# Two softmax mixers of a fused two-stack block: weight low parts from GpSimd to VectorE, the row division from VectorE to ScalarE

## The chip, the cores and the metric

One Trainium2 chip, one core of it. The metric is the device time of one execution of the whole program in microseconds (us). TensorE (PE) does the matmuls, VectorE (DVE), ScalarE (ACT) and GpSimd (POOL) the element-wise work, and SyncE's queue (SP) starts the transfers of the weights.

## The reference

Two stacks of residual blocks run one after the other on a sequence of 256 tokens with 1024 features, batch 1, in float32. The second stack, where the change sits, has four layers. Each layer is a half-weighted gated feed-forward block, an attention mixer, and a second feed-forward block. The mixers of the four layers are, in order, stick-breaking ("sb"), "moba", "mla" and stick-breaking again. With 256 tokens there is one block only, so moba is causal softmax attention with partly rotated queries and keys; mla builds queries and keys through low-rank matrices. Of both mixers what matters here is, for each of 16 heads:

```
logits = q @ k.T * scale            # masked: key position <= query position
p = softmax(logits, axis=-1)        # exp(logits - rowmax) / rowsum
o = p @ v
mix = concat(o) @ w_o
```

## The kernel before

Activations lie transposed, features on partitions. A float32 product is made of three matmuls on parts that TensorE takes at one pass each (`mm3`, lines 343 to 345): high weight part by high activation part, high by low, and low by high. So each weight tile of 128x128 needs two derived tiles. The weights come in chunks of 16 tiles (1 MB) through SP's queue into four buffers named `raw`. Units of 8 tiles are then split: ScalarE rounds `raw` to the high part `whi` (`_hi`, line 295), and a second engine makes the low part `wlo = raw - whi` (`_lo`, line 305). Five buffers each hold `whi` and `wlo`. When the matmuls start a new unit, `ahead` issues the high part of the unit three further on and the low part of the unit two further on (LA is 3). Which engine makes the low part is chosen by `lo_pool`: 0 is VectorE always, 1 is GpSimd always, 2 is every other unit on GpSimd.

A mixer handles two heads at a time, eight pairs in all. `attention` plays an order written out by hand in each slot s (`SLOT`, the entry without a name for moba and mla): `p0 n2 p1 m2 p2 s1 f3`. Here p0 and p1 are the projections of pair s (query and key), n2 is the division by the row sums for pair s-2 (`softmax2`), m2 its transposes on TensorE and the split of the result into `ph` and `pl`, p2 the evacuation of the projections (for moba with the rotation, lines 819 to 823), s1 the scores of pair s-1 and the first half of its softmax (`softmax1`: row maxima on VectorE, four exponentials with row sums on ScalarE into `p` and `sm`), and f3 the product with the values for pair s-3, whose result is split into `xs`. After the eight slots an order named `TAIL` ends the last pairs and begins the output projection. At its first "w" step lo_pool is set to 0 and LA to 1.

The program names the operations in this order; the queue of each engine holds them in nearly this order and runs strictly one after another. An operation that waits holds up all that stands behind it on its engine.

`softmax2` takes one reciprocal of the row sums (128x4) on VectorE (line 869) and then four multiplications by a column of it (line 873): per head 256 columns for the second half of the queries and 128 for the first half. The transposes (line 892) read their result.

Of the kernel before, what the change touches and what calls it, by code (L numbers as in the profile page):

```python
# [12 lines left out]
AF = mybir.ActivationFunctionType  # L13
ALU = mybir.AluOpType
# [194 lines left out]
class Net:  # L209
# [41 lines left out]
    def banks_for(self, attention):  # L251
        one, two = self.ps1, self.ps2
        lin = one[:3] if attention else one
        self.rings = {"lin": lin, "pv": one[3:], "sc": two}
# [612 lines left out]
    def softmax2(self, pool, p, sm):  # L867
        nc = self.nc
        nc.vector.reciprocal(sm, sm)
        for i, sl in enumerate((slice(0, 256), slice(256, 384))):  # L870
            n = sl.stop - sl.start
            for j in range(2):
                nc.vector.tensor_scalar(p[:, j, sl], p[:, j, sl], sm[:, i, j:j + 1], None, op0=ALU.mult)  # L873
        return p

    def softmax2_diff(self, pool, p, sm, l):
# [102 lines left out]
    def attention(self, pool, kind, np_, proj, done, l=0):  # L979

        st = {}
        oset = done
        scale = {"diff": 0.125, "moba": 0.125, "mla": 96 ** -0.5, "sb": 1.0}[kind]

        def score(i):
            qk, rope = st["qk", i]
            if kind == "sb":
                st["sc", i] = self.sb_scores(qk)
                st["sp", i] = self.sb_soft(pool, st["sc", i])
            else:  # L990
                sc = self.scores(i, qk, rope)
                st["p", i] = self.softmax1(pool, sc, scale)

        def norm(i):
            if kind == "diff":
                st["p", i] = self.softmax2_diff(pool, *st["p", i], l)
            elif kind != "sb":
                st["p", i] = self.softmax2(pool, *st["p", i])

        def mid(i):  # L1000
            if kind == "sb":
                st["P", i] = self.sb_tail(pool, st["sc", i], st["sp", i])
            else:
                st["P", i] = self.transposes(pool, i, st["p", i], 1 if kind == "diff" else 2)

        def fin(i):
            if kind == "diff":
                st["o", i] = self.pv_diff(pool, st["P", i], i)
            else:
                oset[i] = self.pv(st["P", i], i)  # L1010

        def sub(i):
            oset[4 + i] = self.subln(*st["o", i], l)

        part = {}

        def w_o(m, upto, tag=None):
            if m not in part:
                b = self.bank(tag) if tag != "sc" else None
                if tag == "sc":  # L1020
                    b = self.bank("sc", 2)[:, 0]
                w, u = [], []
                for _ in range(8):
                    w.append(self.wtile())
                    u.append(self.cur)
                part[m] = [b[:, :S], 0, w, u]
            b, k, w, _ = part[m]
            while k < upto:
                self.mm3(b, w[k], *oset[k], k == 0, k == 7)
                k += 1  # L1030
            part[m][1] = k

        steps = {"n": norm, "f": fin, "m": mid, "s": score, "u": sub}

        def play(order, s):

            for o in order.split():
                if o[0] == "p":
                    proj(s, int(o[1]), st)
                elif o[0] == "v":  # L1040
                    self.vsteps[int(o[1])]()
                elif o[0] == "w":
                    if self.LA > 1:
                        self.lo_pool, self.LA = 0, 1
                    w_o(int(o[1]), int(o[2]), {"": "lin", "s": "sc"}[o[3:]])
                elif s >= int(o[1]):
                    steps[o[0]](s - int(o[1]))

        self.lo_pool = 2 if kind == "diff" else 1
        for s in range(np_):  # L1050
            play(SLOT.get(kind, SLOT[""]), s)
        la = self.LA
        play(TAIL.get(kind, TAIL[""]), np_)
        self.LA = la
        for m in range(8):
            w_o(m, 8, "lin")
            if m < 4:

                first = part[m + 1][3][part[m + 1][1]] if m < 3 else self.cur
                self.ahead(first + 4, first + 3)  # L1060
            self.add_x(m, part[m][0], 1.0)
# [288 lines left out]
```

## Time and profile before

| what | value |
|---|---|
| median of three runs | 2715.5 us (2712.95 to 2717.55) |
| profiled execution | 2710.43 us, its span on the core 2708.7 us |
| busy in the span: PE, DVE, ACT, POOL | 96%, 70%, 51%, 21% |
| mean granted TensorE clock | 0.985 of full speed |
| read from memory | 449.83 MB, 166 GB/s over the span |

The profile takes one execution. Its span is the time from the first to the last instruction on the core. The busy shares are averages over stages that have different limits, so the stages of the two mixers have to be read by themselves. The moba mixer lies at about 1380 to 1495 us of the span, the mla mixer at about 1890 to 1996 us.

### The profile page before, as it was taken

What the parts mean: (1) busy time and instruction counts of PE and PEld (TensorE: products, weight loads), DVE (VectorE), ACT (ScalarE), POOL (GpSimd) and SP (SyncE); (2) the same over time, 40 slices, a digit from 0 to 9 for tenths busy, and PEclk for the clock granted to TensorE, in tenths of its full rate; (3) what the DMA queues carried; (4) which work ended last, traced back from release to release, by engine and by line L of the source; (5) the groups of instructions that cost most, each with busy time, mean ns of one, the idle gap of its engine ahead of it and who ended that gap; (6) DMA issues with size and microseconds to landing.
All of it is one profiled execution on the core that took longest, in us unless ns stands there. A gap on an engine that the chain in (4) does not pass through costs nothing. (4 is left out here: it accounts for less than half of the span.)

```text
span 2708.7 us, 50918 instructions
## 1 busy us (share of the span) xinstructions
PE 2606.3 (96%) x21376; PEld 2547.6 (94%) x21376; DVE 1886.2 (70%) x2615; ACT 1392.5 (51%) x2094; POOL 573.4 (21%) x526
## 2 busy tenths in 40 slices
PE   7899998999999999999998999999899999999998
PEld 6799998999999999999987999999689999989998
DVE  8986599766766576666668765666886666656764
ACT  6544475544544764444445544554554444458553
POOL 6241253313102520010142201002320010143000
PEclk9999999999999999999998999999899999999999
DMA  5255543555555435555542555555235555542552
GB/s 206 98 198 187 172 163 121 191 188 178 173 187 199 141 129 185 187 185 187 192 171 79 176 186 187 185 191 183 71 139 187 186 183 186 188 164 98 196 187 94
DMA packets 64357, 454.15 MB, mean 168 GB/s; under 512 B 7168, under 2 KB 7680, under 8 KB 9984
## 3 DMA queue, kind: packets, MB, share of 16 engines
q1 hardware_dynamic: 63072, 448.16, 47.8%
q8 instruction: 167, 2.74, 0.4%
q0 software_dynamic: 480, 1.57, 0.2%
q10 hardware_dynamic: 576, 1.17, 0.1%
q14 instruction: 62, 0.51, 0.1%
HBM read 449.83 MB, written 1.05 MB: 166 GB/s over the span
## 5 line engine op out<-in xcount | busy, mean ns | idle before, releaser
L295 ACT ACTIVATE whi<-raw 128x1024 fp32r<-128x1024 f32 (+1 forms) x854 | 896.9, 1053 | 765.2 <-PE bank L344 381.0
L305 DVE TENSOR_TENSOR wlo<-raw,whi 128x1024 fp32r<-128x1024 f32 (+1 forms) x787 | 984.3, 1252 | 435.4 <-ACT whi L295 434.5
L343 PE MATMUL bank<-xs,whi 128*128 128x256 f32 x4480 | 1261.7, 282 | 17.8 <-ACT xs L436 16.2
L344 PE MATMUL bank<-xs,whi 128*128 128x256 f32 x4480 | 1261.8, 282 | 13.3 <-DVE xs L437 13.3
L345 PE MATMUL bank<-xs,wlo 128*128 128x256 f32 x4480 | 1260.4, 282 | 3.6 <-DVE wlo L305 3.6
L343 PEld LDWEIGHTS bank<-xs,whi 128*128 128x128 f32 x4480 | 846.5, 189 | 23.1 <-ACT xs L436 18.1
L344 PEld LDWEIGHTS bank<-xs,whi 128*128 128x128 f32 x4480 | 849.4, 190 | 19.0 <-DVE xs L437 17.4
L345 PEld LDWEIGHTS bank<-xs,wlo 128*128 128x128 f32 x4480 | 848.4, 189 | 4.4 <-DVE wlo L305 4.1
L345 PE MATMUL bank<-fh,wlo 128*128 128x256 f32 x1408 | 394.8, 280 | 0.0
L344 PE MATMUL bank<-fl,whi 128*128 128x256 f32 x1408 | 394.8, 280 | 0.0
L343 PE MATMUL bank<-fh,whi 128*128 128x256 f32 x1408 | 394.8, 280 | 0.0
L345 PEld LDWEIGHTS bank<-fh,wlo 128*128 128x128 f32 x1408 | 269.6, 191 | 0.0
L344 PEld LDWEIGHTS bank<-fl,whi 128*128 128x128 f32 x1408 | 264.3, 188 | 0.0
L343 PEld LDWEIGHTS bank<-fh,whi 128*128 128x128 f32 x1408 | 264.3, 188 | 0.0
L445 POOL TENSOR_TENSOR sqt<-x 128x256 f32<-128x256 f32 x124 | 120.4, 971 | 430.0 <-DVE x L668 281.0
L305 POOL TENSOR_TENSOR wlo<-raw,whi 128x1024 fp32r<-128x1024 f32 x67 | 167.5, 2507 | 149.6 <-ACT whi L295 148.2
L442 POOL TENSOR_TENSOR sqacc<-x 128x256 f32<-128x256 f32 x18 | 12.7, 708 | 875.7 <-DVE x L668 663.7
L369 ACT ACTIVATE fh<-act_t 128x256 fp32r<-128x256 f32 x176 | 73.5, 418 | 200.2 <-DVE act_t L727 199.3
L721 DVE TENSOR_TENSOR ffn_t<-bank,rstd 128x512 f32<-128x512 f32 x176 | 121.6, 692 | 64.3 <-PE bank L345 63.9
L344 PE MATMUL bank<-hl,whi 128*128 128x256 f32 x512 | 142.6, 279 | 0.0
L343 PE MATMUL bank<-hh,whi 128*128 128x256 f32 x512 | 142.6, 279 | 0.0
L345 PE MATMUL bank<-hh,wlo 128*128 128x256 f32 x512 | 142.6, 279 | 0.0
(285 smaller groups left out, 2852.9 us busy)
## 6 DMA issues: line engine op xcount, KB each, us to landing
raw<-in_ffn SPq DMA_DIRECT2D x264, 1024.0 KB, 4.8
raw<-in_w SPq DMA_DIRECT2D x100, 1024.0 KB, 4.9
raw<-in_mix SPq DMA_DIRECT2D x59, 1024.0 KB, 4.8
raw<-in_w SPq DMA_DIRECT2D x4, 512.0 KB, 5.6
out_dram<-x SPq DMA_DIRECT2D x4, 256.0 KB, 2.5
raw<-in_w SPq DMA_DIRECT2D x2, 256.0 KB, 4.3
x<-in_xT ACTq DMA_DIRECT2D x2, 256.0 KB, 6.3
x<-in_xT POOLq DMA_DIRECT2D x2, 256.0 KB, 6.5
```

The costliest lines, as they stand in the source:

```text
L295: self.nc.scalar.activation(hi[:, :n * 128], raw, AF.Copy)
L305: eng.tensor_tensor(lo[:, :n * 128], raw, hi[:, :n * 128].bitcast(F32), op=ALU.subtract)
L343: mm(out, lhsT=wh, rhs=xh, start=first, stop=False, **k)
L344: mm(out, lhsT=wh, rhs=xl, start=False, stop=False, **k)
L345: mm(out, lhsT=wl, rhs=xh, start=False, stop=last, **k)
L369: nc.scalar.activation(hi, src, AF.Copy)
L442: eng.tensor_tensor(sq, x, x, op=ALU.mult)
L445: eng.tensor_tensor(t, x, x, op=ALU.mult)
L721: nc.vector.tensor_tensor(t, b, self.rstd[:, None, :].to_broadcast([128, 2, S]), op=ALU.mult)
```

## The change

In `softmax2` the four multiplications by the reciprocal row sums go from VectorE to ScalarE, as a copy with a scale taken from a column (one scale for each partition); the reciprocal stays on VectorE. In `attention` the choice of `lo_pool` changes: mixers of the first stack ("diff") keep 2, stick-breaking keeps 1, and moba and mla get 0 where they had 1, so that VectorE makes every low part there. `softmax2` is called for moba and mla alone.

```
             for j in range(2):
-                nc.vector.tensor_scalar(p[:, j, sl], p[:, j, sl], sm[:, i, j:j + 1], None, op0=ALU.mult)
+                nc.scalar.activation(p[:, j, sl], p[:, j, sl], AF.Copy, scale=sm[:, i, j:j + 1])
         return p
...
-        self.lo_pool = 2 if kind == "diff" else 1
+        self.lo_pool = {"diff": 2, "sb": 1}.get(kind, 0)
         for s in range(np_):
             play(SLOT.get(kind, SLOT[""]), s)
```

## Rows read from the trace of the kernel before

**Rows 1.** Windows: length, busy us (instructions) of PE, PEld, DVE, ACT, POOL; clock, DMA, GB/s

```profile
1000.00:1380.00 380.00, 379.20 (x3179) 377.18 (x3178) 249.30 (x314) 184.21 (x251) 30.96 (x33) 1.00 0.55 189
1380.00:1495.00 115.00, 102.94 (x746) 92.44 (x745) 85.83 (x152) 56.69 (x123) 41.48 (x19) 0.94 0.30 102
1890.00:1996.00 106.00, 89.62 (x684) 79.08 (x684) 84.88 (x180) 54.28 (x132) 30.31 (x20) 0.90 0.21 73
```

**Rows 2.** Waits of PE, 1400 to 1492 us (moba): us in total, times, longest

```profile
PE pair L892 <- DVE p L873: 8.5, 7, 2.4
```

**Rows 3.** Waits of PE, 1900 to 1992 us (mla)

```profile
PE pair L892 <- DVE p L873: 7.5, 8, 1.9
PE bank L343 <- DVE qkt L1182: 4.8, 1, 4.8
```

**Rows 4.** Windows of moba's slots, cut where TensorE ends a pair's projections

```profile
1412.50:1422.90 10.40, 7.94 (x71) 7.31 (x70) 9.11 (x16) 6.13 (x14) 5.40 (x3) 1.00 0.31 102
1422.90:1463.00 40.10, 32.97 (x225) 29.37 (x225) 31.75 (x56) 19.20 (x51) 15.16 (x7) 0.83 0.23 79
1463.00:1472.70 9.70, 8.79 (x76) 8.03 (x73) 9.15 (x18) 6.03 (x14) 1.23 (x1) 1.00 0.32 110
1466.90:1475.90 9.00, 9.00 (x78) 8.32 (x77) 8.46 (x19) 6.05 (x14) 0.00 (x0) 1.00 0.27 86
```

**Rows 5.** Windows of mla: its entry, the first scores, the slots after them

```profile
1901.30:1921.30 20.00, 12.31 (x71) 10.39 (x71) 19.20 (x31) 8.69 (x17) 12.72 (x8) 0.85 0.31 105
1921.30:1932.90 11.60, 10.37 (x68) 8.72 (x68) 7.09 (x18) 4.66 (x14) 2.38 (x1) 0.67 0.29 106
1932.90:1980.40 47.50, 41.28 (x341) 35.23 (x342) 38.42 (x98) 27.62 (x77) 4.75 (x2) 0.93 0.07 25
```

**Rows 6.** Timeline of POOL at 1437 us: start, us, engine, line, operation

```profile
1437.77 4.75 POOL L305 TENSOR_TENSOR wlo<-raw,whi 128x1024 fp32r<-128x1024 f32 x2 [9.99 <-ACT whi L295]
```

**Rows 7.** Timeline of DVE at four places, one of them beside the row of POOL

```profile
1437.75 2.48 DVE L873 TENSOR_SCALAR p<-p,sm 128x128 f32<-128x128 f32 x1
...
1465.56 0.68 DVE L822 TENSOR_TENSOR ropes<-ropes,tabr 128x512 f32<-128x512 f32 x1
...
1472.23 0.75 DVE L873 TENSOR_SCALAR p<-p,sm 128x256 f32<-128x256 f32 x3
...
1963.74 0.42 DVE L822 TENSOR_TENSOR ropes<-ropes,Sq 128x256 f32<-128x256 f32 x1
```

**Rows 8.** DVE by line, 1380 to 1496 us: count, busy us, mean ns, idle before

```profile
L873 DVE TENSOR_SCALAR p<-p,sm 128x256 f32<-128x256 f32 (+1 forms) x32 | 17.4, 595 | 0.4
L822 DVE TENSOR_TENSOR ropes<-ropes,tabr 128x512 f32<-128x512 f32 x8 | 11.6, 1452 | 0.0
L823 DVE TENSOR_TENSOR qkt<-qkt,ropes 128x512 f32<-128x512 f32 x8 | 8.4, 1052 | 0.0
```

**Rows 9.** DVE by line, 1890 to 1998 us

```profile
L873 DVE TENSOR_SCALAR p<-p,sm 128x256 f32<-128x256 f32 (+1 forms) x32 | 10.5, 379 | 0.1
L822 DVE TENSOR_TENSOR ropes<-ropes,Sq 128x256 f32<-128x256 f32 x4 | 4.7, 1164 | 0.2 <-POOL Sq L1156 0.2
L823 DVE TENSOR_TENSOR act_s<-act_s,ropes 128x256 f32<-128x256 f32 x5 | 3.9, 780 | 0.0
L459 DVE TENSOR_TENSOR rt<-ry 128x256 f32<-128x256 f32 (+1 forms) x3 | 3.0, 999 | 0.5 <-ACT ry L378 0.5
L822 DVE TENSOR_TENSOR ropes<-ropes,ffn_t 128x256 f32<-128x256 f32 x1 | 2.6, 2639 | 0.0
```

**Rows 10.** Line 305 between 1000 and 1200 us: min/median/max ns

```profile
L305 DVE TENSOR_TENSOR wlo<-raw,whi x72: 1207/1225/1245, 999.5 to 1199.3; 128x1024 fp32r<-128x1024 f32 x72
```

**Rows 11.** ACT: groups of the whole span, and its timeline at 1436 us

```profile
L421 ACT ACTIVATE x<-x,vec 128x256 f32<-128x256 f32 x8 | 4.0, 502 | 14.8 <-DVE sqt L445 14.8
L378 ACT ACTIVATE p<-pair,mx 128x128 f32<-128x128 f32 x48 | 17.2, 369 | 0.0
...
1436.63 1.06 ACT L295 ACTIVATE whi<-raw 128x1024 fp32r<-128x1024 f32 x1
```

More of the change, by code (lines that the diff above doesn't have):

```diff
@@ L872, in softmax2 @@
             for j in range(2):
-                nc.vector.tensor_scalar(p[:, j, sl], p[:, j, sl], sm[:, i, j:j + 1], None, op0=ALU.mult)
+                nc.scalar.activation(p[:, j, sl], p[:, j, sl], AF.Copy, scale=sm[:, i, j:j + 1])
         return p
@@ L1047, in play @@
                     steps[o[0]](s - int(o[1]))
-        self.lo_pool = 2 if kind == "diff" else 1
+        self.lo_pool = {"diff": 2, "sb": 1}.get(kind, 0)
         for s in range(np_):
```

## The prediction, on record before the changed kernel ran

> **What bounds the kernel now.** I first read the windows of whole stages. Between the two mixers TensorE is busy 379.2 of 380 us at full clock; nothing that other engines do there can cost time. Inside the mixers it is busy 102.9 of 115 us and 89.6 of 106, at a mean granted clock of 0.94 and 0.90 [rows 1]. So the change can only be worth what TensorE loses in these two places: 12 + 16 us without a matmul, and the slow stretches on top.
>
> Then TensorE's own waits. In moba the largest is the first transpose of a pair, waiting for the divided `p` of line 873: 8.5 us in 7 waits [rows 2]. In mla it is the same wait, 7.5 us in 8, and one single wait of 4.8 us for the evacuated queries and keys [rows 3]. All of these end on VectorE.
>
> Then the slots. From 1466.9 to 1475.9 stands one moba slot (projections, transposes, scores, values) with 9.0 us of matmuls in 9.0 us, at clock 1.00, and with GpSimd idle [rows 4]. The three slots in the 40.1 us before 1463.0 hold the same work with GpSimd making low parts, and take 13.4 us each at a clock of 0.83; the one after them takes 9.7 [rows 4]. The first slot, still without a value product, has 7.94 us of work in 10.4.
>
> Last, why VectorE is late. At 1437.77 GpSimd begins two `wlo` [rows 6]; the multiplication of 128 columns that VectorE begins at 1437.75 lasts 2.48 us [rows 7], against 0.75 us for three of them where GpSimd is idle [rows 7]. Line 822, with two inputs in SBUF, takes 0.68 us undisturbed (0.42 at half the width) [rows 7] and 1.45 on average in moba [rows 8]. So each `wlo` of GpSimd can stop VectorE for the best part of its own length, and it hits the very step that TensorE waits for.
>
> **The change part by part.** *Low parts leave GpSimd.* What goes are the stalls, mean minus undisturbed, times count. Moba: line 873, 32 x 0.595 less 16 x 0.35 and 16 x 0.27 (estimated from the three in 0.75 us, which overlap, and their likes at both widths) = 9.1; line 822, 8 x (1.45 - 0.68) = 6.2; line 823, same shape, 8 x (1.05 - 0.68) = 3.0 [rows 7, 8]. Together 18.3 us. Mla: line 873, 32 x 0.379 - 9.9 = 2.2; line 822, 4 x (1.16 - 0.42) + (2.64 - 0.42) = 5.2; line 823, 5 x (0.78 - 0.42) = 1.8; line 459, 3.0 less an estimated 1.0 for its three = 2.0 [rows 7, 9]. Together 11.2. Sum: 29.5 us of VectorE.
>
> *Low parts come to VectorE.* One takes 1.23 us there [rows 10]. Moba's eight pairs have 128 projection tiles, 16 units; mla's have 52 tiles, and the units looked up in its slots are 7. 23 x 1.23 = 28.3 us. So VectorE's time for the low parts is nearly the same as the stalls. What differs is the place: the queue puts each `wlo` at the start of a unit, and it is the one for two units on, whose `whi` was issued a unit earlier; a stall falls wherever GpSimd happens to be. The clean slot shows that the place is good: its VectorE made low parts itself, 8.46 us busy, and no matmul was late [rows 4].
>
> *The multiplications leave VectorE.* 64 of them at 0.25 us (three in 0.75) [rows 7] = 16 us less in its queue.
>
> *They come to ScalarE.* The trace has the same operation at 256 columns, line 421: 0.50 us; for 128 columns the nearest is the exponential with a column operand, 0.37 [rows 11]. Four cost 2 x 0.50 + 2 x 0.37 = 1.74 us end to end, and not less than the 1.0 us of VectorE; I take 1.5, since consecutive ones overlap. ScalarE then goes from 56.7 to some 69 of 115 us and from 54.3 to 66 of 106 [rows 1]: not full. On the path to the transposes it adds 1.5 - 1.0 = 0.5 us, at most 0.74. It also adds a place in a queue: at 1436.63, behind the exponentials, stands a `whi` of 1.06 us [rows 11], which the division could pass on VectorE and can't on ScalarE. Behind the division stand the next `whi`, the `ph` split and the `xs` copies.
>
> *What does not change.* No transfer is added. SP's queue waits for low parts to free `raw`; the DMA share is only 0.30 and 0.21 [rows 1], so a `raw` freed a microsecond later is covered. If that cover were gone, a late chunk would cost a `whi` and hence up to a slot's slack.
>
> *Weighed against a rule.* The row shows 29.5 us of stalls for low parts that cost 28.3 us on VectorE [rows 7 to 10]. The Trainium skill, "Perfetto Trace Analysis", section "Optimizing Scalar/DVE Operations", says that GpSimd and VectorE share a port into SBUF, so that moving work between the two might not help. By that rule the first half of the change is worth about nothing; by the place of the stalls it is worth most of the sum below.
>
> **The sum.** Moba slots: 10.4 - 7.94, 40.1 - 3 x 9.0 and 9.7 - 9.0 make 2.5 + 13.1 + 0.7 = 16.3 us over the clean slot [rows 4], clock loss included. Against that the later division: six transposes at 0.6 us (0.15 for the longer first piece, and a `whi` ahead of it in about half of the slots, 0.5), 3.6. The last two pairs in the tail have little else for TensorE: 2 x 0.4 = 0.8. Moba: 12 us.
>
> Mla's entry, 1901 to 1921: VectorE is busy 19.2 of 20 us [rows 5], and the stalls in it are 2.2 (line 822), 2.0 (line 459) and two of about 2 (lines 822 and 823), about 8 [rows 9]; one low part of 1.23 comes in: 6.9. TensorE has 12.3 us of work there, so it allows 7.7. I take 6.5, most of it the 4.8 us wait [rows 3]. Next stretch: 11.6 us at clock 0.67, about 3.8 us lost to the clock [rows 5]; the low clock follows the long wait, so I take 2.5 back. Slots after: 47.5 us with two low parts of GpSimd, one long wait of 1.9 us [rows 3, 5], which goes; the division on ScalarE costs 7 x 0.5 = 3.5 there, since mla's pairs have less TensorE work to hide it. Mla: 6.5 + 2.5 + 1.9 - 3.5 = 7.4, rounded 7.
>
> Together 19 us: 2710.4 - 19 = 2691 for the profiled execution. That execution lies 5 us below the median of the runs shown; from the median the forecast is 2715.5 - 19 = 2696.5. Bounds: without any later division and with all of the clock back, 16.3 + 6.9 + 3.8 + 1.9 = 29 us, 2686.5; with 1.06 + 0.74 = 1.8 us at each of 16 pairs, 28.8 us lost, nothing left.
>
> **The rivals.** *ScalarE's queue takes half back.* Every division stands behind a whole `whi`: 1.06 + 0.5 instead of 0.6 or 0.5 us at 13 pairs, 13 us more lost. For it: the row at 1436.63 [rows 11]. Against: moba's slot has an estimated 6 to 7 us of matmuls between the scores and the transposes (9.0 less those two themselves). Gain 6: 2709.5.
>
> *The stalls only change their name.* 28.3 us of low parts stand in VectorE's queue where 29.5 us of stalls stood, ahead of the same rotations and maxima, and the transposes wait as before; the 16 us saved by the division is idle time. For it: the equal sums. Against: the clean slot. 2715.5, within 5 us. This is the time that the rule of the Trainium skill ("Perfetto Trace Analysis", "Optimizing Scalar/DVE Operations") would give.
>
> *Slower: the two queues lock.* A `whi` stands behind a division that waits for VectorE's reciprocal; the `wlo` that needs it then waits at the head of VectorE's queue and holds the next reciprocal. VectorE breaks even while each `wlo` waits less than (29.5 + 16 - 28.3) / 23 = 0.75 us. From there it costs 23 us for each further microsecond; at a whole `whi` and half of another, 1.6 us, 20 us, less what the mixers' slack of about half takes: about 10 slower, 2725. For it: strict queues. Against: the low part lags its high part by a unit.
>
> *It does what it says but the clock stays low*, so that only the waits are saved: about 19 - 6 = 13, 2702.5; that lies inside the forecast's own case.
>
> **How the numbers follow.** This kernel's measurement can tell 0.2%, 5.4 us, from no change. Chances: forecast (with the clock variant) 0.62, own range 2687 to 2706; ScalarE's queue 0.14, mostly faster by more than 5.4; same name 0.12; locked queues 0.12. Faster: 0.62 + 0.12 = 0.74. Same: 0.02 + 0.11 = 0.13. Slower: 0.13. The range, from the lower bound to the upper edge of the case without effect but for its last part, is 2686 to 2717: some 0.95 of the first, all of the second and half of the third, 0.79.
>
> **What would show it.** Right: GpSimd has no `wlo` in the two mixers; VectorE's lines 822 and 823 are at 0.68 us throughout in moba; moba's slots are 9 to 10 us long at clock 1.0; the 4.8 us wait in mla is under 1 us; the transposes' waits are now named after ScalarE's `p`, under 1 us each. Wrong: transposes that wait over 1 us for ScalarE with a `whi` just ahead of the division; `wlo` on VectorE waiting for `whi` inside the slots; or clean VectorE durations with slots still 11 us long.

## The result, and the profile after

| kernel | median, us (runs) | ratio to before, 95% interval |
|---|---|---|
| before | 2716.38 (2712.95 to 2717.55, 4 runs) | 1 |
| changed | 2683.65 (2676.58 to 2686.21, 4 runs) | 0.9893 [0.9867, 0.9919] |

The change makes the kernel faster by 1.1%. Taken from the median of the runs shown that is 0.9893 x 2715.5 = 2686.4 us, a gain of 29, where 2696.5 and a gain of 19 were forecast: right in direction, short in size, 0.4 us inside the lower bound of 2686. The profiled execution went from 2710.43 to 2686.21 us, 24.2 less.

The page of the changed kernel, busy time in the span, us (share) xinstructions:

```profile
span 2684.4 us, 50850 instructions
...
PE 2602.4 (97%) x21376; PEld 2544.1 (95%) x21376; DVE 1865.9 (70%) x2574; ACT 1413.7 (53%) x2158; POOL 518.2 (19%) x503
```

VectorE's share is still 70%, the figure from before. Over the whole span nothing tells why 24 us are gone.

To see where they went one needs marks that both kernels have. GpSimd's first square of a feed-forward block's input (line 442) is one: it starts when the block ahead is done. The timeline of GpSimd in the changed kernel (start, us, engine, line, operation, [idle before]) at the two marks around moba:

```profile
1319.76 0.61 POOL L442 TENSOR_TENSOR sqacc<-x 128x256 f32<-128x256 f32 x1 [10.51 <-DVE x L668]
1486.16 0.61 POOL L442 TENSOR_TENSOR sqacc<-x 128x256 f32<-128x256 f32 x1 [100.16 <-DVE x L666]
```

Windows cut at such marks hold the feed-forward block ahead of a mixer and the mixer. Moba's and mla's, in the kernel before (length, busy us of PE, PEld, DVE, ACT, POOL, clock, DMA, GB/s):

```profile
1316.91:1494.93 178.02, 165.96 (x1244) 153.75 (x1243) 121.79 (x193) 84.33 (x157) 55.59 (x33) 0.96 0.39 133
1830.11:1995.66 165.55, 149.17 (x1189) 138.58 (x1187) 118.32 (x217) 79.85 (x162) 44.15 (x35) 0.94 0.33 113
```

and in the changed kernel:

```profile
1319.76:1486.16 166.40, 163.17 (x1247) 150.53 (x1246) 114.43 (x177) 95.14 (x189) 16.62 (x17) 1.00 0.41 142
1821.83:1971.77 149.94, 143.62 (x1191) 133.51 (x1190) 106.68 (x192) 90.05 (x194) 27.45 (x28) 1.00 0.36 125
```

Moba gains 11.6 us, mla 15.6: 27.2 together. The same matmuls take 2.8 and 5.5 us less (165.96 to 163.17 and 149.17 to 143.62), the clock being 1.00 for 0.96 and 0.94; the other 8.8 and 10.1 us are time in which TensorE no longer stands idle. VectorE has 19.0 us less to do in the two (240.1 to 221.1), for 17.2 forecast (29.5 of stalls and 16 of divisions less 28.3).

The unchanged code ahead of moba took 2.85 us more in this execution (1319.76 for 1316.91), the stretches between and behind came out within 0.5 us: with the 27.2 that makes the 24.3 by which the span is shorter. A second profile of the changed kernel (e7 below) gives 11.5 and 15.6 again, while its unchanged part ahead of moba differs by 8 us from the first. So below, gains are read from these marks as well as from the runs. They have a limit too: the unchanged stretch just ahead of mla's (third to fourth mark) takes 187.0 us in ten of the fourteen profiles and 184.9 in four, so a difference under 2 us counts only where several profiles repeat it.

Now moba's slots. Windows of the changed kernel, the second one three slots, the last two mla's entry and mla's slots:

```profile
1408.10:1423.10 15.00, 14.55 (x133) 13.71 (x132) 13.93 (x26) 10.79 (x27) 0.00 (x0) 1.00 0.43 141
1423.10:1451.30 28.20, 27.96 (x225) 25.21 (x224) 23.95 (x46) 21.66 (x55) 0.00 (x0) 1.00 0.33 113
1460.80:1486.20 25.40, 22.94 (x168) 19.47 (x167) 14.60 (x29) 15.18 (x43) 0.04 (x1) 1.00 0.12 42
...
1893.00:1913.00 20.00, 19.12 (x149) 16.59 (x148) 19.45 (x48) 11.73 (x22) 3.16 (x4) 1.00 0.38 125
1913.00:1966.00 53.00, 48.22 (x407) 41.24 (x406) 40.11 (x88) 43.58 (x130) 0.00 (x0) 1.00 0.17 59
```

Three slots take 28.2 us, 9.4 each, at clock 1.00, where they took 13.4 at 0.83 [rows 4]; 9.0 was the clean one. Of the 20 us at mla's entry TensorE is busy 19.1 where it was 12.3, at clock 1.00 for 0.85 [rows 5]. GpSimd is idle in the slots. What is left is the tail of moba (third line): 22.9 us of matmuls in 25.4.

TensorE's waits in the changed kernel, first 1390 to 1480 us, then 1860 to 1975 (us in total, times, longest):

```profile
PE pair L892 <- ACT p L873: 2.3, 4, 1.1
...
PE pair L892 <- ACT p L873: 4.6, 8, 1.0
PE bank L343 <- DVE qkt L1182: 0.9, 1, 0.9
```

The first transpose now waits for ScalarE's `p`: 2.3 us in moba for 8.5 [rows 2], 4.6 in mla for 7.5 [rows 3]. The one wait of 4.8 us is down to 0.9 [rows 3].

And VectorE by line, changed kernel, 1380 to 1486 us (count, busy us, mean ns, idle before):

```profile
L305 DVE TENSOR_TENSOR wlo<-raw,whi 128x1024 fp32r<-128x1024 f32 x23 | 28.2, 1228 | 10.4 <-ACT whi L295 10.3
...
L823 DVE TENSOR_TENSOR qkt<-qkt,ropes 128x512 f32<-128x512 f32 x8 | 5.5, 683 | 0.0
L822 DVE TENSOR_TENSOR ropes<-ropes,tabr 128x512 f32<-128x512 f32 x8 | 5.5, 682 | 0.0
```

Lines 822 and 823 take 0.68 us in every slot, for 1.45 and 1.05 [rows 8]. The 10.3 us in which VectorE stood idle ahead of `wlo`, waiting for `whi`, are looked at below.

### The profile page after: what moved, and what is told of

It reads as the page before. It is cut to its first block, busy times and chain, and to the rows that moved or that the text cites. A ratio compares the mean times of both kernels' runs of the same rounds, so it can differ in the third digit from the quotient of the medians.

```text
span 2684.4 us, 50850 instructions
## 1 busy us (share of the span) xinstructions
PE 2602.4 (97%) x21376; PEld 2544.1 (95%) x21376; DVE 1865.9 (70%) x2574; ACT 1413.7 (53%) x2158; POOL 518.2 (19%) x503
## 3 DMA queue, kind: packets, MB, share of 16 engines
HBM read 449.83 MB, written 1.05 MB: 168 GB/s over the span
## 4 chain that ended last, share of the span: by engine, by line
PE 72%; DVE 7%; ACT 3%; issue 1%; POOL 1%; DVEq 0%; ACTq 0%; POOLq 0%
PE bank L343 22%; PE bank L345 22%; PE bank L344 22%; DVE wlo L305 2%; ACT p L378 1%; DVE xs L437 1%; PE bank L790 1%; PE bank L792 1%; PE bank L793 1%; PE pair L848 1%; ACT whi L295 0%; DVE x L666 0%; ACT p L873 0%; PE bank L908 0%; PE pair L969 0%
## 5 line engine op out<-in xcount | busy, mean ns | idle before, releaser
L305 DVE TENSOR_TENSOR wlo<-raw,whi 128x1024 fp32r<-128x1024 f32 (+1 forms) x810 | 1011.4, 1250 | 448.1 <-ACT whi L295 446.8
L343 PE MATMUL bank<-xs,whi 128*128 128x256 f32 x4480 | 1262.9, 283 | 19.5 <-ACT xs L436 16.3
L442 POOL TENSOR_TENSOR sqacc<-x 128x256 f32<-128x256 f32 x18 | 12.8, 708 | 968.1 <-DVE x L668 666.0
L446 POOL TENSOR_TENSOR sqacc<-sqacc,sqt 128x256 f32<-128x256 f32 x124 | 133.0, 1072 | 9.4
```

The lines of the kernel that those rows point to most:

```text
L305: eng.tensor_tensor(lo[:, :n * 128], raw, hi[:, :n * 128].bitcast(F32), op=ALU.subtract)
L343: mm(out, lhsT=wh, rhs=xh, start=first, stop=False, **k)
L446: i = eng.tensor_tensor(sq, sq, t, op=ALU.add)
```

## The experiments

The theory: it is the *low parts leaving GpSimd* that bring the gain, since GpSimd's subtractions stopped VectorE at places that TensorE waits for; the division on ScalarE costs a little. The rivals: the gain comes from VectorE's freed 16 us of divisions; the stalls are harmless and something else in GpSimd's queue was slow (its own 2.4 us for a low part, say); or GpSimd disturbs by being busy at all. A further one is in the traces: TensorE's queue does not have the same order in all of these kernels. In mla the first transpose stands behind 21 projection tiles before the change and behind 25 in the changed kernel.

Ratios are to the kernel before, with 95% intervals; stage gains are moba / mla from the marks.

| kernel | median, us | ratio | moba / mla, us |
|---|---|---|---|
| e1_low_only | 2679.74 | 0.9885 [0.9871, 0.9898] | -14.7 / -17.1 |
| e2_div_only | 2712.81 | 0.9996 [0.9983, 1.0009] | +0.2 / +1.9 |
| e3_spare | 2711.4 | 0.9994 [0.9982, 1.0006] | +2.4 / -2.3 |
| e4_mla_entry | 2691.48 | 0.9924 [0.9907, 0.9942] | -11.6 / -8.4 |
| e5_sb_vector | 2679.76 | 0.9891 [0.9873, 0.991] | -15.0 / -17.1 |
| e6_all_vector | 2666.47 | 0.984 [0.9821, 0.9858] | -14.9 / -17.1 |
| e7_changed_again | 2683.17 | 0.9906 [0.9887, 0.9926] | -11.5 / -15.6 |
| e8_one_head | 2682.27 | 0.9903 [0.9886, 0.992] | -12.0 / -15.2 |
| e9_mla_late | 2684.05 | 0.9905 [0.9888, 0.9923] | -11.6 / -12.0 |
| e10_spare_write | 2683.83 | 0.9905 [0.9882, 0.9929] | -12.8 / -15.0 |
| e11_all_one_head | 2668.94 | 0.9848 [0.9828, 0.9868] | -12.0 / -15.2 |
| e12_spare_write_paced | 2686.11 | 0.9903 [0.9877, 0.9929] | -11.5 / -15.4 |

### Each half by itself

e1_low_only, against the changed kernel: low parts on VectorE, the division stays there too.

```
-                nc.scalar.activation(p[:, j, sl], p[:, j, sl], AF.Copy, scale=sm[:, i, j:j + 1])
+                nc.vector.tensor_scalar(p[:, j, sl], p[:, j, sl], sm[:, i, j:j + 1], None, op0=ALU.mult)
```

> Only the low parts go from GpSimd to VectorE; the division stays on VectorE. Theory A (the stalls of VectorE beside GpSimd are what cost, and the later division on ScalarE gives a little back): all of the gain or more, 24 to 36 us faster than the kernel before, so within 5 us of the changed kernel or up to 8 us faster than it; the transposes wait for VectorE's p under 3 us in moba. Theory B (what counts is that VectorE's queue gets shorter by the 16 us of the multiplications): the low parts alone bring 28 us into that queue for 29 us of stalls, so a third of the gain at most, 0 to 10 us faster than before.

e2_div_only, against the changed kernel: the division on ScalarE, low parts on GpSimd as before.

```
-        self.lo_pool = {"diff": 2, "sb": 1}.get(kind, 0)
+        self.lo_pool = 2 if kind == "diff" else 1
```

> Only the division goes to ScalarE; GpSimd still makes the low parts. Theory A: the stalls that hit line 873 (11 us of VectorE's time in both mixers) go, those of lines 822, 823 and 459 stay and some move to other two-input operations; 3 to 12 us faster than before, and mla's entry keeps a wait of 3 us or more for the evacuated queries and keys. Theory B: most of the gain, 18 us or more faster than before.

e1 has the whole gain, 0.9885, and e2 none, 0.9996: for e2 even theory A, with 3 to 12 us, was too high. In e1 the transposes wait 3.8 us for `p` in moba, a little over the 3 that were expected. The windows of the two stages in e1:

```profile
1316.59:1479.92 163.33, 159.39 (x1244) 149.44 (x1243) 121.44 (x209) 84.85 (x157) 16.62 (x18) 1.00 0.42 145
1815.17:1963.63 148.46, 141.80 (x1189) 133.09 (x1188) 113.31 (x224) 79.17 (x162) 27.44 (x28) 1.00 0.37 126
```

VectorE is busy 234.7 us in them for 240.1 before, and the stages are 31.8 us shorter. So the gain is not a lighter load of VectorE. Whether the order of TensorE's queue, which e1 changes as well, has a part in it, e1 can't tell; e3 below bears on that.

Why e2 has none although the stopped instruction left VectorE is seen on VectorE by line, e2, 1380 to 1496 us, and in TensorE's waits there, in moba (first) and mla (the last two):

```profile
L822 DVE TENSOR_TENSOR ropes<-ropes,tabr 128x512 f32<-128x512 f32 x8 | 14.7, 1837 | 0.0
...
L823 DVE TENSOR_TENSOR qkt<-qkt,ropes 128x512 f32<-128x512 f32 x8 | 13.3, 1663 | 0.2
```

```profile
PE pair L892 <- ACT p L873: 8.9, 7, 3.0
...
PE pair L892 <- ACT p L873: 9.1, 9, 2.7
PE bank L343 <- DVE qkt L1182: 5.3, 1, 5.3
```

The stall goes on to the next instructions that GpSimd can stop: line 822 from 1.45 to 1.84 us, line 823 from 1.05 to 1.66. Over undisturbed 0.68 that is 8 x 1.16 + 8 x 0.98 = 17.1 us, for the 18.3 that lay on three lines before. The waits of the transposes are as long as they were in moba (8.9 for 8.5) and longer in mla (9.1 for 7.5), with ScalarE's name on them. Moving the stopped instruction away did not end the stall here; the next ones had it.

### The stalls put back

e3_spare keeps all of the change, and GpSimd makes each difference of moba's and mla's slots once more, in two pieces, into a tile that nobody reads. So nothing waits for GpSimd's result, though the buffers that it reads are held longer. If the gain goes, it was the disturbance.

```
+        if self.spare:
+            for c in (slice(0, 512), slice(512, n * 128)):
+                t = self.st([128, 512], "ffn_t")[:, :c.stop - c.start]
+                self.nc.gpsimd.tensor_tensor(t, raw[:, c], hi[:, c].bitcast(F32), op=ALU.subtract)
...
+        self.spare = kind in ("moba", "mla")
```

> The changed kernel with a spare subtraction on GpSimd beside each low part that VectorE makes in the slots of moba and mla (the same 1024 columns from SBUF in two pieces of 512, result never read). No engine waits for the spare result. Theory A: GpSimd's accesses stop VectorE again whoever makes the low part, so lines 822 and 823 rise from 0.68 to over 1 us on average and 12 us or more of the gain is lost; with VectorE's 28 us of low parts on top the time may come back to that of before, 2700 to 2725 us. Rival C (the gain came from the place of the low parts in the order, from who waits for whom, and not from the stalls): within 5 us of the changed kernel.

All of it goes: 0.9994. VectorE by line in e3, 1380 to 1510 us (its lines lie 4 further down, so 826 is 822), and the spare subtractions on GpSimd:

```profile
L305 DVE TENSOR_TENSOR wlo<-raw,whi 128x1024 fp32r<-128x1024 f32 x27 | 39.2, 1453 | 10.8 <-ACT whi L295 10.5
L826 DVE TENSOR_TENSOR ropes<-ropes,tabr 128x512 f32<-128x512 f32 x8 | 10.4, 1296 | 0.0
L827 DVE TENSOR_TENSOR qkt<-qkt,ropes 128x512 f32<-128x512 f32 x8 | 8.0, 997 | 0.0
```

```profile
L309 POOL TENSOR_TENSOR ffn_t<-raw,whi 128x512 f32<-128x512 f32 x32 | 55.9, 1778 | 24.5 <-ACT whi L295 22.9 <-issue 1.6
```

The rotations are slow again, and `wlo` itself now is (1.45 for 1.23 us): 8 x 0.62 + 8 x 0.32 + 27 x 0.225 = 13.6 us of stalls on these three lines. e3 is not the kernel before with the names changed, since VectorE carries the low parts and the stalls; that both come out at the same time is a coincidence of size.

By the traces TensorE and VectorE run these two stages in the same order in e3 as in the changed kernel, so the order alone doesn't bring the gain: the stages are 14.0 and 13.3 us longer with it. Buffers held longer are a small part at most: in moba ScalarE waits once, 1.8 us, for a `whi` that GpSimd still reads, and the transfers wait 19.8 us for GpSimd, 4.1 at the longest, where they wait 71.4 us for VectorE's low parts (112.7 in the changed kernel).

e10_spare_write and e12_spare_write_paced ask whether any work on GpSimd does it. Each low part is joined by four fills of 512 columns of a tile that nobody reads: GpSimd then only writes. In e10 nothing held the fills back, and the moba ones ran in one piece ahead of the slots, so e12 puts a copy of one column of `whi` ahead of each four.

```
+        if self.spare:
+            self.nc.gpsimd.tensor_copy(self.st([128, 512], "ffn_t")[:, 0:1], hi[:, 0:1].bitcast(F32))   # e12 alone
+            for _ in range(4):
+                self.nc.gpsimd.memset(self.st([128, 512], "ffn_t"), 0.0)
```

> The changed kernel with four memsets of 512 columns on GpSimd beside each low part, so that GpSimd is as busy as with the spare subtraction but reads nothing. If VectorE stops whenever GpSimd works in SBUF: as slow as with the spare subtraction, 2700 us or more. If it is the reading that collides (the Trainium skill, SBUF - State Buffer, section Who interferes with whom, says so of a VectorE operation with two inputs in SBUF): lines 822 and 823 stay at 0.68 us and the time within 5 us of the changed kernel.

> In the run before, the memsets waited for nothing and ran ahead: 32 of them in one piece before moba's slots. Here a copy of one column of the high part stands ahead of each four memsets on GpSimd, which paces them to one group of 2.1 us for each low part, all through the slots. If any work of GpSimd in SBUF stops VectorE: 12 us or more slower than the changed kernel, lines 822 and 823 over 1 us on average. If only reading collides: those lines within 0.05 us of 0.68 and the time within 5 us of the changed kernel (2684 us, 0.990 of before).

GpSimd by line in e12, 1400 to 1480 us, and under it VectorE by line, 1380 to 1496:

```profile
L309 POOL MEMSET ffn_t<- 128x512 f32 x58 | 30.5, 526 | 3.4
L307 POOL COPY ffn_t<-whi 128x1 f32<-128x1 f32 x14 | 9.0, 644 | 14.8 <-ACT whi L295 14.8
```

```profile
L827 DVE TENSOR_TENSOR qkt<-qkt,ropes 128x512 f32<-128x512 f32 x8 | 5.5, 682 | 0.0
L826 DVE TENSOR_TENSOR ropes<-ropes,tabr 128x512 f32<-128x512 f32 x8 | 5.4, 679 | 0.0
```

GpSimd is busy for half of the time in the slots, and VectorE's rotations don't notice: 0.68 us, ratio 0.9903, the changed kernel's. TensorE and VectorE have the same order in e12 and e3. So what stops these two-input operations is not that GpSimd is busy or writes; what its subtractions have beyond the fills is that they *read*. For the one-input division of the kernel before no run has fills beside it on VectorE. The Trainium skill, "SBUF — State Buffer", section "Who interferes with whom", says this of two inputs: a VectorE instruction with two inputs in SBUF contends with a GpSimd instruction that reads SBUF, not with one that only writes. The rows agree: 0.68 us beside fills, 1.30 and 1.00 beside subtractions.

### Where in mla

e4_mla_entry gives the low parts of mla's first three slots back to GpSimd, e9_mla_late those of the later ones.

```
+            if kind == "mla":
+                self.lo_pool = 1 if s < 3 else 0      # e4; in e9: 0 if s < 3 else 1
```

> The changed kernel with GpSimd making the low parts again in mla's slots 0 to 2 alone, where its entry and first scores lie. Theory A, with the entry as the place where mla gained more than forecast: 8 to 14 us slower than the changed kernel, the wait of 3 to 5 us for the evacuated queries and keys back, and the granted clock under 0.9 in the 25 us after it. Rival D (mla's gain was spread over its eight pairs): within 4 us of the changed kernel.

> The complement of the run with GpSimd in mla's first slots: the changed kernel with GpSimd making mla's low parts from slot 3 on, some four of them, and VectorE making those of the entry. If the two halves of mla add up: 6 to 9 us slower than the changed kernel in the mla stage, of which 8 us are left when the entry is disturbed. If the slots after the entry hide their stalls, as the prediction half assumed (1.9 us there): under 3 us slower.

Three low parts in the entry, 1894 to 1910 us, cost 15.6 - 8.4 = 7.2 us of the stage, 2.4 each and a little under the 8 that were expected; the four of e9, which GpSimd made from 1902.6 on, 15.6 - 12.0 = 3.6, 0.9 each. In the runs e9 can't be told from the changed kernel, and e4's interval overlaps with the changed kernel's. TensorE's waits in mla in e4:

```profile
PE pair L892 <- ACT p L873: 4.4, 6, 1.2
PE bank L343 <- DVE qkt L1184: 3.4, 1, 3.4
```

The single wait for `qkt` is 3.4 us again, for 0.9 in the changed kernel and 4.8 before [rows 3]. In e9 it is 3.0: its first low part lies beside the entry, so e9 doesn't leave the entry alone. A clock under 0.9 behind it was expected in e4 and didn't come: the windows from 1893 to 1913 and on to 1935 show 0.97 and 0.95.

A mark inside the stage tells more. The first 717 matmuls of it are the same ones in all of these kernels: the feed-forward block, the value projections, 19 query and key tiles but for one matmul, and the first pair's scores. The stage split there, in us:

| kernel | first 717 matmuls | the rest |
|---|---|---|
| before | 99.1 | 66.4 |
| changed | 87.9 | 62.0 |
| e1_low_only | 87.9 | 60.5 |
| e2_div_only | 99.0 | 68.5 |
| e3_spare | 95.2 | 68.0 |
| e4_mla_entry | 95.4 | 61.8 |
| e9_mla_late | 91.5 | 62.0 |

e4 and e9 lose all that they lose in the first part. In the rest they are as fast as the changed kernel, although GpSimd makes two of e9's four low parts there. The two losses sum to 10.8 of the 17.5 us that separate e2 (+1.9) from the changed kernel (-15.6). In the first part they add up to e2's (7.5 and 3.6 for 11.1); what is missing lies in the rest, 68.5 for 62.0. The rest is slow only in the three kernels in which GpSimd subtracts for all of the stage's units (before, e2, e3). Why two low parts there cost nothing in e9 stays open; the order of TensorE's queue, which differs between e9 and e2, was not separated from it.

### The division

e7_changed_again is the changed kernel once more; e8_one_head leaves head 0 on VectorE and gives head 1 to ScalarE.

```
-                nc.scalar.activation(p[:, j, sl], p[:, j, sl], AF.Copy, scale=sm[:, i, j:j + 1])
+                if j == 0:
+                    nc.vector.tensor_scalar(p[:, j, sl], p[:, j, sl], sm[:, i, j:j + 1], None, op0=ALU.mult)
+                else:
+                    nc.scalar.activation(p[:, j, sl], p[:, j, sl], AF.Copy, scale=sm[:, i, j:j + 1])
```

> The changed kernel again, beside the others on one chip, to price the division on ScalarE against the kernel with the low parts alone. Theory A (the prediction's step: later divisions cost 7 to 8 us): 4 to 8 us slower than the low parts alone. Theory B (the shorter queue of VectorE is worth something): as fast or faster.

> The low parts on VectorE, the division of a pair's first head on VectorE and of its second on ScalarE, side by side. Theory A: the first transposes start as early as with VectorE alone and the last piece is ready 0.3 to 0.5 us sooner, so 0 to 4 us faster than the low parts alone; if ScalarE's queue (a high part ahead of the division) sets the last piece, as slow as the changed kernel.

By the runs the three places of the division can't be told apart: 0.9885, 0.9906 and 0.9903, with intervals that overlap. By the marks they can. With the division on VectorE moba gains 14.7, 15.0 and 14.9 (e1, e5, e6), with it on ScalarE 11.5 to 12.8 (changed, e7, e10, e12); mla gains 17.1 each time against 15.0 to 15.6. The division on ScalarE thus costs 3.1 us in moba and 1.5 in mla, and sharing it saves nothing of that (12.0 and 15.2).

In moba the cost lies in the tail. ScalarE's timeline there, changed kernel:

```profile
1470.58 0.51 ACT L873 ACTIVATE p<-p,sm 128x256 f32<-128x256 f32 x1 [1.24 <-DVE mx L860]
...
1472.72 1.89 ACT L873 ACTIVATE p<-p,sm 128x256 f32<-128x256 f32 x5
```

and the same stretch of VectorE's in e1, with its tail as a window:

```profile
1467.66 0.17 DVE L869 RECIPROCAL sm<-sm 128x4 f32<-128x4 f32 x1
...
1467.87 1.01 DVE L873 TENSOR_SCALAR p<-p,sm 128x256 f32<-128x256 f32 x4
```

```profile
1458.00:1479.90 21.90, 21.03 (x164) 18.93 (x164) 16.50 (x42) 10.99 (x31) 0.00 (x0) 1.00 0.14 49
```

In e1 the four pieces of the last pair but one follow on the reciprocal at once, while ScalarE makes the last pair's exponentials. In the changed kernel one piece runs, then the four exponentials of the last pair, all in one queue, and only then the other three pieces: they start 2.1 us after the first. From the last pair's reciprocal to the mark are 13.3 us in the changed kernel (1472.87 to 1486.16) and 10.1 in e1 (1469.79 to 1479.92): the 3.1 us of the stage.

### The low parts that GpSimd still makes

e5_sb_vector is e1 with the stick-breaking mixers' low parts on VectorE too (`{"diff": 2}.get(kind, 0)`), e6_all_vector is e1 with none on GpSimd anywhere (`self.lo_pool = 0`), e11_all_one_head is e6 with the division shared as in e8.

> Low parts of moba, mla and also both stick-breaking mixers on VectorE, the division on VectorE too. Theory A: what can be won is what TensorE loses in a mixer; in the first stick-breaking mixer that is under 4 us of 140, at full clock, so 0 to 6 us faster than with the low parts of moba and mla alone (2674 to 2680 us against that run's 2680). Rival: any low part taken from GpSimd is worth about 1.3 us, as the 23 of moba and mla were, so the 32 of stick-breaking bring 30 us or more.

> As the run before it, and the low parts of the first stack's mixers on VectorE too, so none is left on GpSimd. Theory A: 12 more low parts, 15 us more for a VectorE that is busy 87% of the first of these mixers, against stalls of the same size; TensorE idles 12 us of 122 there, for waits on the scan as well: between 3 us slower and 5 us faster than the run before it. Rival as before: 15 us faster.

> No low part on GpSimd in any mixer, and the division shared, one head on VectorE and one on ScalarE. From the runs before, the sharing is worth nothing against VectorE alone: as fast as the kernel with all low parts on VectorE (0.984 of before), within 4 us. If VectorE, now with all low parts, is the one that TensorE waits for, the shared division is 3 to 6 us faster than that.

In stick-breaking it is worth nothing: 0.9891 beside e1's 0.9885. In the first stack, where I expected next to nothing, it is worth 2679.76 - 2666.47 = 13.3 us, for twelve low parts, six in each of two mixers by e5's trace. The first of these mixers as a window, and VectorE by line in it, before:

```profile
60.00:128.00 68.00, 55.41 (x402) 50.81 (x400) 61.47 (x119) 36.03 (x86) 17.16 (x11) 0.90 0.27 93
```

```profile
L881 DVE TENSOR_SCALAR p<-p,sm 128x256 f32<-128x256 f32 (+1 forms) x8 | 4.9, 652 | 0.0
L822 DVE TENSOR_TENSOR ropes<-ropes,tabr 128x512 f32<-128x512 f32 x4 | 4.5, 1116 | 1.1 <-POOL tabr L1079 1.1
L1275 DVE TENSOR_SCALAR xp<-r 128x256 f32<-128x256 f32 x2 | 2.7, 1376 | 0.0
```

and in e6, the same mixer, 60 to 122 us:

```profile
60.00:122.00 62.00, 52.56 (x407) 47.53 (x406) 59.39 (x124) 37.38 (x87) 6.00 (x9) 0.97 0.30 102
```

```profile
L881 DVE TENSOR_SCALAR p<-p,sm 128x256 f32<-128x256 f32 (+1 forms) x8 | 2.6, 371 | 0.0
...
L1275 DVE TENSOR_SCALAR xp<-r 128x256 f32<-128x256 f32 x2 | 0.5, 264 | 0.0
```

It is moba's picture in small: the division at 0.65 us for 0.37, the clock at 0.90 for 0.97, and some 6 us more for the same work, 402 and 407 matmuls in the records. I had counted these low parts as few and had not read the clock there. e6 is the fastest kernel found: 0.984 [0.9821, 0.9858], ahead of e11 (0.9848, not told apart) and of the change.

## Why the prediction was right in direction and 10 us short

e1 and the changed kernel split the stages into the prediction's own two terms.

| term | forecast, us | measured, us |
|---|---|---|
| low parts, moba | 16.3 | 14.7 (e1) |
| low parts, mla | 6.5 + 2.5 + 1.9 = 10.9 | 17.1 (e1) |
| division, moba | -3.6 - 0.8 = -4.4 | -3.1 (changed less e1) |
| division, mla | -3.5 | -1.5 |
| sum | 19 | 27 |

**Right: place, not sum.** The low parts cost 1.23 us each on VectorE, as the prediction had it, and its busy time in the two stages fell by 19.0 us with the divisions gone and by 5.4 with them still there (e1). The rival that the stalls only change their name, which the prediction also drew from the rule of the Trainium skill ("Perfetto Trace Analysis", "Optimizing Scalar/DVE Operations") that moving work between these two engines might not help, would have given 2715.5; measured 0.9893, and e1 0.9885. The equal sums are true and don't decide: e1 has nearly the same sum and is 31.8 us shorter in the two stages. e3 shows that GpSimd's subtractions take the gain away again, with no result of theirs waited for and TensorE's queue in the changed kernel's order.

**Right: moba's slots.** 9.4 us at clock 1.00 for a forecast between 9 and 10; the 4.8 us wait at 0.9 for "under 1"; lines 822 and 823 at 0.68 throughout. The waits of the transposes reach 1.1 us where under 1 was said.

**Luck: the range.** 2686.4 us lies 0.4 above its lower bound, and not by the bound's reasoning. The bound took the division at nothing and the low parts at 29 us; measured are 4.6 and 31.8, two misses that go opposite ways.

**Off: the division, 7.9 forecast, 4.6 measured.** Six late transposes at 0.6 us were too many: TensorE waits 2.3 us for them in moba in all. The tail was taken at 0.8 and holds about all of the 3.1, since I had counted the longer instructions and not the exponentials that stand in the same queue. In mla 3.5 was taken and 1.5 measured.

**The failed step: mla's slots after the entry.** For them the prediction added a wait of 1.9 us that goes and a division that costs 3.5: 1.6 us longer. They came out 4.4 us shorter. The prediction's cut, the first transpose at 1932.9, isn't at the same work in both kernels, since the order of TensorE's queue differs. So mla is cut here at the first matmul behind the wait for `qkt` and again after 717 matmuls, before:

```profile
1830.11:1921.30 91.19, 83.50 (x675) 81.53 (x673) 64.18 (x83) 41.49 (x57) 37.01 (x31) 0.97 0.48 166
1921.30:1929.23 7.93, 7.93 (x43) 6.75 (x44) 3.76 (x8) 2.77 (x7) 0.40 (x1) 0.51 0.36 136
1929.23:1995.66 66.43, 57.73 (x474) 50.30 (x472) 50.38 (x126) 35.59 (x102) 6.74 (x4) 0.95 0.11 36
```

and in the changed kernel:

```profile
1821.83:1905.16 83.33, 82.45 (x675) 81.09 (x673) 56.54 (x84) 41.39 (x56) 27.45 (x27) 1.00 0.49 170
1905.16:1909.76 4.60, 4.60 (x43) 3.92 (x44) 4.60 (x8) 2.40 (x4) 0.00 (x0) 1.00 0.45 142
1909.76:1971.77 62.01, 56.57 (x476) 48.50 (x475) 45.54 (x102) 46.26 (x136) 0.00 (x1) 1.00 0.18 63
```

The first two stretches gain 7.9 and 3.3 us, 11.2 for the 9.0 that were forecast (6.5 + 2.5): 6.8 us less without a matmul, and 4.4 us of shorter matmuls, since the clock was at 0.51 in the second stretch and below 1.00 in the first. The third gains 4.4: 3.3 us less without a matmul, and 1.2 of shorter matmuls, for which the prediction had counted nothing at 0.93 [rows 5]. Its two terms are split by e1, whose third stretch takes 60.5 us. The low parts are worth 5.9 there (66.4 to 60.5) where I took 1.9, the longest wait alone; the division costs 1.5 (60.5 to 62.0) where I took 3.5. Together they are the 6.0 us between +1.6 and -4.4. The waits of the transposes, all in this stretch, fell from 7.5 to 4.6 us although their division went to the slower engine. Which of GpSimd's low parts had made them longer stays open: in e9 two in the same stretch cost nothing.

**The rivals.** ScalarE's queue taking half back: a whole `whi` does stand ahead of the division in the timeline below, yet the slots are 9.4 us long, 0.4 over the clean one. Locked queues: 2725 was wrong, but its condition was nearly met. ScalarE's and then VectorE's timeline in a moba slot of the changed kernel:

```profile
1431.02 1.07 ACT L295 ACTIVATE whi<-raw 128x1024 fp32r<-128x1024 f32 x1
1431.97 1.49 ACT L873 ACTIVATE p<-p,sm 128x256 f32<-128x256 f32 x4
1433.35 1.05 ACT L295 ACTIVATE whi<-raw 128x1024 fp32r<-128x1024 f32 x1
```

```profile
1432.12 1.23 DVE L305 TENSOR_TENSOR wlo<-raw,whi 128x1024 fp32r<-128x1024 f32 x1 [0.77 <-ACT whi L295]
```

The division takes 1.49 us (1.5 forecast) behind a `whi` and ahead of the next one. `wlo` waits 0.77 us for that `whi`, at the break-even of 0.75 that the prediction gave; all such idle time in moba's stretch is 10.3 us over 23 low parts, 0.45 each. The slots are full of matmuls all the same (27.96 of 28.2), so it is idle time of an engine that isn't the bound. A `wlo` waiting for its `whi` inside the slots was one of the signs named for being wrong; it is there, and the slots are within 0.4 us of the clean one. *The clock stays low* fell as well: 1.00 in every window of the changed kernel above.

## What to carry to other kernels

Before moving work between two engines that disturb each other, look past the sum of busy times to where in the in-order queue the cost lands: 28 us of low parts at the head of a unit left the slots full of matmuls here, and without the 29 us of stalls the two stages were 31.8 us shorter (e1). Moving the stopped instruction away instead was worth nothing, since the next one was stopped in its place (e2). When a stage also shows a granted clock under 1.00, add that loss over the whole stage, not only over the stretch of the longest wait, and look for the same signs in every other stage that does the same thing: twelve low parts that were passed over were worth 13 us (e6). And cut a stage where both kernels have done the same work: an instruction that two builds queue in different places, as the first transpose here, is no such mark.

## What the runs showed of the hardware that was not expected

- GpSimd at work for half of the time leaves VectorE's two-input operations at 0.68 us if it fills tiles, with a copy of one column ahead of each four fills (e12); one that subtracts tiles stretches them to 1.30 and 1.00 us (e3).
- Operations with one tensor input were stopped too beside GpSimd's subtractions: 2.48 us for 128 columns [rows 7], and line 1275 at 1.38 us for 0.26 without them.
- GpSimd's own time varied as well: its spare subtractions of 512 columns in moba took 1.27 us at the least, 1.78 on average and 2.34 at the most (e3). That VectorE stopped them is argued, not shown.
- One and the same code ahead of moba took 1319.76 us in one profile of the changed kernel and 1312.06 in another, while the stage behind it agreed to 0.1 us.
